# An encoder trunk: Strassen's seven products for most of the down projection, with the weight sums made in memory

## The chip, the cores and the metric

The kernel runs on one core of one Trainium2 chip. The metric is the device time of one execution in microseconds. One execution was profiled; the profile's times are counted from the start of its span.

## What is computed

Two layers of an encoder over 512 tokens of width 1024, in float32. Each layer is an attention and convolution half, an output projection, and a feed-forward half. The change is in the last line of the layer: the product of the gated activations (512 x 2816) with `w_down` (2816 x 1024).

```python
for l in range(DEPTH):                                  # DEPTH = 2
    h = rms_norm(x, pre_mix_norm[l])
    proj = jnp.einsum('bsd,de->bse', h, w_in[l])         # 1024 -> 3072: q, k, v, conv_u, gate_b, gate_c
    ...
    mix = jnp.einsum('bse,ed->bsd', merged, w_out[l])    # 1024 -> 1024
    x = x + rms_norm(mix, post_mix_norm[l])
    h = rms_norm(x, pre_ffn_norm[l])
    g, u = jnp.split(jnp.einsum('bsd,df->bsf', h, w_gate_up[l]), 2, axis=-1)   # 1024 -> 2 x 2816
    f = jnp.einsum('bsf,fd->bsd', jax.nn.silu(g) * u, w_down[l])               # 2816 -> 1024
    x = x + rms_norm(f, post_ffn_norm[l])
```

## The kernel before, in words

**Arithmetic.** Every float32 operand of a large product is split into a high part, rounded to the format that TensorE takes, and a low part, the rest. ScalarE (ACT) makes the high part with a copy and VectorE (DVE) the low part with a subtraction. A product is then three matmuls: high by high, high by low, low by high (`mm3`, L204 to L206).

**Weights.** They come from memory in an order fixed on the host, in chunks of 128 x 2048; half a chunk (128 x 1024, 512 KB) is the unit. `load_raw` (L117) loads a half into one of three "raw" buffers by SyncE's (SP's) queue. `split_half` splits it (ACT L177, DVE L178) into one of four pairs of buffers "wh" and "wl", after asking for the next two raw halves. `take` returns a half for use and splits up to two further ones.

**Order.** The program is traced under a planner. `tc.manual_schedule` holds only TensorE (PE) and SP to the order of the program. For ACT, DVE and GpSimd (POOL) the planner takes, at each moment of its own simulation, the instruction that stands first in the program among those whose inputs and buffers it believes to be ready; what comes out is a fixed list for each engine, which the chip runs in order, each instruction waiting for the semaphores that it needs. A few instructions are pinned with `keep_in_program_order` (the loading of ACT's tables, L119 and L235), and in the first stage ACT and DVE are held too.

**Stages of a layer.** (1) In-projection, with attention and convolution interleaved. Before it, in layer 0, `first_values` works with the first weights as they come: the loads stand in `LOADS`, positions, transposed x, weights, then x itself, whose squares (L543) give the norm (L222 and on); meanwhile POOL makes the angles of the rotary embedding from the positions (`rotary_values`, L285 to L315). In the attention and convolution steps, the square of each finished tile of 128 features is added to a running sum by POOL (L396), from a "tmp" tile, of which there are four; a convolution (`conv_tile`) holds two of them at once. (2) Out-projection: evacuations L674 to L678, norm, gain (L248), transposes into the next operand (L255 to L262). Here the first weights of the next stage are split by two DMAs of POOL's queue, a plain one (L189) and one that adds to what lies in the tile (L191). (3) Gate and up projections: 22 tiles of 128 hidden features; the first four by ordinary products, the other 18 by Strassen's seven products (`seven`, L815 to L855, its matmuls at L827 with 256 columns), whose weight sums DVE makes in SBUF (`prepare`). (4) Down projection: feature half f = 0, then 1; the contraction runs over 22 tiles m, for four token tiles t at once, with one bank of PSUM each; the last 4 (f = 0) or 8 (f = 1) tiles m run token tile by token tile, so that the evacuation of one (`evac`, ACT L918, DVE L920) lies under the matmuls of the next. Activations are split here (`split`, ACT L709, DVE L710), up to four tiles m ahead. With f = 1 the rest of the layer follows for each token tile: norm, residual (L643), the next layer's norm and gain, and the transposes of the first two token tiles (L255), placed three tiles m into the products of token tile t + 2.

**Buffers that matter here.** Eleven "big" tiles of 8 KB a partition, four "tmp", three "mid", two "gain", two "kl", and in PSUM four banks "acc", three "att", one "pv".

Of the kernel before, what the change touches and what calls it, by code (L numbers as in the profile page):

```python
# [16 lines left out]
F32 = mybir.dt.float32  # L17
# [13 lines left out]
MT = FFN // P  # L31
NCHUNK = 49
EPS = 1e-6
# [5 lines left out]
RAW_AHEAD, LOOK, WBUFS = 2, 2, 4  # L39

NDIRECT = 2

# [34 lines left out]
@with_exitstack  # L77
def encoder(ctx: ExitStack, tc: tile.TileContext, x, xT, pos, mask, cols, rows, w, out):
    nc = tc.nc
# [31 lines left out]
    def load_raw(i, c=0, d=1024):  # L111

        if i >= 2 * DEPTH * NCHUNK:
            return
        if i not in raws:
            raws[i] = sb.tile([P, 1024], F32, tag="raw", bufs=RAW_AHEAD + 1, name=nm("raw"))
        nc.sync.dma_start(raws[i][:, c:d], w[i // 2][:, (i % 2) * 1024 + c:(i % 2) * 1024 + d])  # L117

# [18 lines left out]

    def load_row(l, i):
        g = sb.tile([P, D], F32, tag="gain", bufs=2, name=nm("gain"))
        nc.sync.dma_start(g, rows[l, i].partition_broadcast(P))  # L140
        return g
# [38 lines left out]
    def split_by_dma(l, h):  # L180


        src = w[l * NCHUNK + 16][:, h * 1024:h * 1024 + 1024]
# [5 lines left out]
        nc.gpsimd.dma_start(hi, src)  # L189
        nc.scalar.activation(lo, hi.bitcast(F32), AF.Copy, scale=-1.0)  # L190
        nc.gpsimd.dma_start(lo, src, accum_op=ALU.add)  # L191
        halves[2 * (l * NCHUNK + 16) + h] = (hi, lo)

    def take(n, h, keep=None):


        i = 2 * n + h
# [355 lines left out]

    def in_proj_attention(l, hT, h, tables):

# [140 lines left out]

    def feed_forward(l, hT, hs, raw):
        base = l * NCHUNK + 16
# [7 lines left out]

        def split(m, src):
            hi, lo = act_dst(m)
            nc.scalar.copy(hi, src)  # L709
            nc.vector.tensor_sub(lo, src, hi.bitcast(F32))  # L710

        def unsplit(m):

            i = m - NDIRECT
            if i < 8:
                key, make, k = i // 4, lambda: big([P, 4, S]), i % 4
            elif i < 12:
                key, make, k = i // 2, lambda: sb.tile([P, 2, S], F32, tag="gain", bufs=2, name=nm("gain")), i % 2
            elif i < 18:
                key, make, k = i // 2, lambda: mid([P, 2, S]), i % 2  # L720
            else:
                key, k = i, 0
                make = lambda: sb.tile([P, 1, S], F32, tag="u" if i == 18 else "sqa", bufs=1, name=nm("u"))
            if key not in stage:
                stage[key] = make()
            return stage[key][:, k, :]

        def gated(m, gate, up):

            if m < NDIRECT:  # L730
                nc.vector.tensor_mul(gate, up, gate)
                split(m, gate)
            else:
                nc.vector.tensor_mul(unsplit(m), up, gate)

# [47 lines left out]
        def prepare(m):  # L783
# [23 lines left out]
            yield  # L807

        def down_splits():
            for k in (0, None, 1, None, 2, None):  # L810
                if k is not None:
                    split_half(2 * (l * NCHUNK + 38) + k)
                yield
# [83 lines left out]
        dbase = l * NCHUNK + 38  # L897
        fx = [[None] * NT for _ in range(2)]
# [3 lines left out]
        hs = [None] * NT  # L902
        done = set()

        def down(f, m, t, acc, keep=None):
            if m >= NDIRECT and m not in done:
                split(m, unsplit(m))
            done.add(m)
            u = f * MT + m
            wh, wl = take(dbase + u // 4, (u % 4) // 2, keep)  # L910
            c = (u % 2) * 512
            hi, lo = act_dst(m)
            mm3(acc, hi[:, t * P:(t + 1) * P], lo[:, t * P:(t + 1) * P], wh[:, c:c + 512], wl[:, c:c + 512],
                m == 0, m == MT - 1)

# [7 lines left out]
        for f in range(2):  # L923
            accs = [bank("acc") for _ in range(NT)] if f == 0 else [bank(g) for g in ("att", "att", "att", "pv")]
            tail = 4 if f == 0 else 8
            for m in range(MT - tail):
                if f == 0:
                    for k in range(m, min(m + 4, MT)):
                        if k >= NDIRECT and k not in done:
                            split(k, unsplit(k))  # L930
                            done.add(k)
                    if m == 14 - 3:
                        gpost = load_row(l, 3)
                        gnext = load_row(l + 1, 0) if l + 1 < DEPTH else None
                for t in range(NT):
                    down(f, m, t, accs[t])
            if f == 1 and gnext is not None:
                hT = new_hT()
            for t in range(NT):
                for m in range(MT - tail, MT):  # L940
                    if m == MT - tail + TURN_D and f == 1 and gnext is not None and t >= 2:
                        transposed(t - 2, hs[t - 2], hT, "acc")
                        hs[t - 2] = None
                    down(f, m, t, accs[t], 2 * dbase + (f * MT + MT - tail) // 2 if t < NT - 1 else None)
                evac(f, t, accs[t])
                if f == 0:
# [11 lines left out]
    with tc.manual_schedule(engines={mybir.EngineType.PE, mybir.EngineType.SP}):  # L958
# [4 lines left out]
        for l in range(DEPTH):  # L963
            merged, sq_a, sq_c, tables, inv = in_proj_attention(l, hT, hs, tables)
            hT, hs, raw = out_proj(l, merged, sq_a, sq_c, inv)
            hT, hs = feed_forward(l, hT, hs, raw)


def _weight_chunks(w_in, w_out, w_gate_up, w_down):

    out = np.empty((DEPTH * NCHUNK, P, 2048), np.float32)
    n = 0
    for l in range(DEPTH):
# [24 lines left out]
        wd = w_down[l].reshape(MT, P, 2, 512).transpose(2, 0, 1, 3).reshape(2 * MT, P, 512)  # L998
        for c in range(11):
            chunks.append(wd[4 * c:4 * c + 4].transpose(1, 0, 2).reshape(P, 2048))  # L1000
        for c in chunks:
            out[n] = c
            n += 1
    return out

# [44 lines left out]
```

## Time and profile before

| | us |
|---|---|
| median of 3 runs (1176.79 to 1177.01) | 1176.98 |
| the profiled execution, its own time | 1176.98 |
| its span | 1175.2 |
| TensorE (PE) busy | 1162.7 |
| weight loads (PEld) busy | 1025.1 |
| DVE busy | 784.0 |
| ACT busy | 630.0 |
| POOL busy | 41.6 |

A row of the page's groups, or of the same view for a stretch, reads: source line, engine, operation, output<-input by the program's names, shapes, count | busy time in us, mean ns of one | idle time of the engine ahead of them, and what ended most of it. The view of stretches gives, for each stretch, the busy time and number of instructions of PE, PEld, DVE, ACT and POOL, the granted TensorE clock, the mean busy share of the 16 DMA engines, and GB/s. A row of the timeline has the start, the duration, engine, line, and in brackets the idle time before it and what ended it. A row of DMA issues ends in the median time from issue to landing; a row of DMA queues has packets, MB, and the time that the packets took as a share of 16 engines. Matmuls overlap, so the mean of one (about 390 ns at 512 columns) is longer than the step from one to the next.

### The profile page before, as it was taken

The page shows a single profiled execution, that of the slowest core. Times are in us where ns is not written, and L with a number is a line of the kernel's source. Part 1 is how long each engine was busy: PE and PEld are TensorE (multiplying, and loading weights), DVE is VectorE, ACT ScalarE, POOL GpSimd, SP SyncE. Part 2 cuts the span into 40 slices and gives each one's busy share as a digit, 9 for nine tenths or more (in the row PEclk, how much of TensorE's full clock was granted, in tenths as well). Part 3 has the DMA queues.
Part 4 walks back from the last instruction along what each step waited for, and adds up shares of the span by engine and source line. Part 5 has one row for each costly group of instructions (what it writes and reads, how often), then busy time and mean ns, then how long its engine had stood idle before and what let it go on. Part 6 is the DMA issues. An engine that isn't in the chain of part 4 may idle for free.

```text
span 1175.2 us, 18024 instructions
## 1 busy us (share of the span) xinstructions
PE 1162.7 (99%) x7096; PEld 1025.1 (87%) x7096; DVE 784.0 (67%) x1326; ACT 630.0 (54%) x1217; POOL 41.6 (4%) x63
## 2 busy tenths in 40 slices
PE   9999999999999999999999999999999999999997
PEld 8777778899999999888877777788999999998886
DVE  5798655777888887432557986448778888883323
ACT  6677544654656557331445775437546555582211
POOL 6000011000000000000000000100000000000000
PEclk9999999999999999999999999999999999999999
DMA  8221234122333333423132212442133233334221
GB/s 321 90 72 54 73 94 135 60 73 90 108 108 102 99 107 116 154 74 118 42 106 92 72 55 73 128 123 71 38 108 106 95 106 108 108 126 125 90 72 72
DMA packets 33781, 116.48 MB, mean 99 GB/s; under 512 B 4000, under 2 KB 4000, under 8 KB 33696
## 3 DMA queue, kind: packets, MB, share of 16 engines
q1 hardware_dynamic: 31824, 110.05, 29.0%
q0 software_dynamic: 1152, 4.19, 1.6%
q8 instruction: 55, 0.90, 0.3%
q10 hardware_dynamic: 720, 1.09, 0.3%
q14 instruction: 30, 0.25, 0.1%
HBM read 113.22 MB, written 2.10 MB: 98 GB/s over the span
## 4 chain that ended last, share of the span: by engine, by line
PE 90%; DVE 4%; ACT 2%; POOL 2%; issue 2%; DVEq 0%; POOLq 0%
PE acc L827 18%; PE att L827 13%; PE acc L204 12%; PE acc L205 12%; PE acc L206 12%; PE att L204 4%; PE att L206 4%; PE att L205 4%; PE pv L441 3%; PE att L434 2%; PE att L417 1%; PE att L418 1%; PE pv L206 1%; PE pv L205 1%; PE pv L204 1%
## 5 line engine op out<-in xcount | busy, mean ns | idle before, releaser
L178 DVE TENSOR_TENSOR wl<-raw,wh 128x1024 fp32r<-128x1024 f32 x116 | 141.6, 1221 | 165.3 <-ACT wh L177 164.7
L177 ACT CAST wh<-raw 128x1024 fp32r<-128x1024 f32 x116 | 121.7, 1051 | 176.7 <-PE acc L206 67.4
L827 PE MATMUL acc<-big,wh 128*128 128x256 f32 x1152 | 212.0, 283 | 0.0
L827 PEld LDWEIGHTS acc<-big,wh 128*128 128x128 f32 x1152 | 179.8, 192 | 0.2
L827 PE MATMUL acc<-big,wl 128*128 128x256 f32 x576 | 163.0, 283 | 0.0
L827 PE MATMUL att<-big,wh 128*128 128x256 f32 x864 | 160.3, 283 | 0.0
L204 PE MATMUL acc<-big,wh 128*128 128x512 f32 (+1 forms) x400 | 154.1, 385 | 0.0
L206 PE MATMUL acc<-big,wl 128*128 128x512 f32 (+1 forms) x400 | 149.6, 374 | 0.0
L205 PE MATMUL acc<-big,wh 128*128 128x512 f32 (+1 forms) x400 | 149.3, 373 | 0.0
L827 PEld LDWEIGHTS att<-big,wh 128*128 128x128 f32 x864 | 134.7, 192 | 0.2
L827 PE MATMUL att<-big,wl 128*128 128x256 f32 x432 | 122.2, 283 | 0.0
L778 DVE TENSOR_TENSOR wl<-t,wh 128x1024 fp32r<-128x1024 f32 x72 | 88.0, 1222 | 42.7 <-ACT wh L777 42.7
L777 ACT CAST wh<-t 128x512 fp32r<-128x512 f32 x144 | 89.0, 619 | 47.6 <-PE att L827 31.7
L827 PEld LDWEIGHTS acc<-big,wl 128*128 128x128 f32 x576 | 110.6, 192 | 0.0
L204 PE MATMUL acc<-wh,big 128*128 128x512 f32 x272 | 106.6, 392 | 0.0
L205 PE MATMUL acc<-wl,big 128*128 128x512 f32 x272 | 106.0, 390 | 0.0
L206 PE MATMUL acc<-wh,big 128*128 128x512 f32 x272 | 105.9, 389 | 0.0
L204 PE MATMUL att<-wh,big 128*128 128x512 f32 x228 | 89.4, 392 | 0.0
L206 PE MATMUL att<-wh,big 128*128 128x512 f32 x228 | 88.8, 390 | 0.0
L205 PE MATMUL att<-wl,big 128*128 128x512 f32 x228 | 88.8, 389 | 0.0
L206 PEld LDWEIGHTS acc<-big,wl 128*128 128x128 f32 x400 | 75.3, 188 | 14.0
L204 PEld LDWEIGHTS acc<-big,wh 128*128 128x128 f32 x400 | 75.4, 189 | 12.3 <-issue 0.8
(238 smaller groups left out, 2100.8 us busy)
## 6 DMA issues: line engine op xcount, KB each, us to landing
raw<-in_w SPq DMA_DIRECT2D x188, 512.0 KB, 3.7
gain<-in_rows SPq DMA_DIRECT2D x7, 512.0 KB, 5.9
big<-in_xT SPq DMA_DIRECT2D x8, 256.0 KB, 5.3
raw<-in_w SPq DMA_DIRECT2D x8, 256.0 KB, 5.3
x<-in_x SPq DMA_DIRECT2D x4, 512.0 KB, 6.9
wk<-in_w POOLq DMA_DIRECT2D x4, 512.0 KB, 6.0
big<-in_w POOLq DMA_DIRECT2D x4, 512.0 KB, 4.9
out_dram<-x SPq DMA_DIRECT2D x4, 256.0 KB, 2.1
```

Source lines behind the costliest of these rows:

```text
L177: nc.scalar.copy(hi, raws[i])
L178: nc.vector.tensor_sub(lo, raws[i], hi.bitcast(F32))
L204: nc.tensor.matmul(o, sh, mh, start=start, stop=False)
L205: nc.tensor.matmul(o, sh, ml, start=False, stop=False)
L206: nc.tensor.matmul(o, sl, mh, start=False, stop=stop)
L417: nc.tensor.matmul(sc, qk[:, hd, q0:q0 + P], qk[:, 2 + hd, :], start=True, stop=False)
L418: nc.tensor.matmul(sc, qk[:, hd, q0:q0 + P], kl[:, hd, :], start=False, stop=True)
L434: nc.tensor.transpose(tp[:, k * P:(k + 1) * P], sm[:, k * P:(k + 1) * P], ident)
L441: nc.tensor.matmul(o[hd * 64:hd * 64 + 64, half * 256:half * 256 + 256], V[:, k, hc:hc + 64], PT[hd][:, k, :], start=k == 0, stop=k == NT - 1)
L777: nc.scalar.copy(hi[:, c:c + 512], src[:, c:c + 512])
L778: nc.vector.tensor_sub(lo[:, :n], src[:, :n], hi[:, :n].bitcast(F32))
L827: nc.tensor.matmul(o[:, :HS], sh[:, c], mh[:, k, :], start=start and k == 0 and n == 0, stop=k == 3 and n == 2, skip_group_check=True)
```

## The change

The 22 contraction tiles of the down projection are divided: tiles 0 to 15 go by Strassen's scheme in Winograd's form, tiles 16 to 21 (`REST` = 6) as before. The 16 tiles make a product of a 2 x 2 block of activations (token half by contraction half) with a 2 x 2 block of weights b11, b12, b21, b22 (contraction half by feature half). Seven products of 8 tiles, for 2 token tiles each, replace eight; each is `partial`, 8 x 2 x 3 matmuls of 512 columns. The ones after the first add to banks into which ACT or DVE has copied an earlier result; `written` runs a matmul on a bank ahead of such a copy.

- **Weights.** `w_down` gets an array of its own, `wd`, laid out by quarters. A layer has 34 halves for the down projection instead of 22: 28 for the products (`SB`), six for the rest. Four of the seven products take sums of weight quarters, t1 = b11 + b12, t3 = b12 + b22, t2 = t1 + b22, t4 = t2 + b21, which are read from a tensor in memory, `tsum`.
- **Sums.** `weight_sums` makes them by 16 DMAs a layer from memory to memory, of 1 MB each, issued by POOL: eight copies and eight with `accum_op=add`. It is a generator: the program takes one step of it in every eighth `advance` of the attention stage, one after each of the 18 gate/up tiles, and what is left after the last.
- **Activations.** `gated` no longer splits tiles 0 and 1 at once; all tiles are kept unsplit (`place`). For each product `operands` makes the sum of activation quarters where one is needed (four of seven, DVE), the high part (ACT) and the low part (DVE), in three pieces, under the product before; the first set under the last gate/up tile, with the first weight splits. Tiles 16 to 21 are split under the seventh product.
- **The end.** After the seven products the eight banks hold both feature halves; the six remaining tiles are added token tile by token tile, 18 matmuls each, with the evacuation, norm and transposes as before.
- **Gains.** `gpost` and `gnext` are loaded at the head of the stage, into the "kl" tiles, not at its eleventh tile.

```diff
+    tsum = [dpool.tile([P, 4, KS * 512], F32, tag=f"tsum{l}", name=f"tsum{l}") for l in range(DEPTH)]
...
+    def weight_sums(l):
+        b11, b12, b21, b22 = (down_quarter(l, g, f) for g in range(2) for f in range(2))
+        t1, t2, t3, t4 = (tsum[l][:, k, :] for k in range(4))
+        for pairs in (((t1, b11), (t3, b12)), ((t1, b12), (t3, b22)), ((t2, t1),), ((t2, b22),), ((t4, t2),), ((t4, b21),)):
+            for n, (o, src) in enumerate(pairs):
+                for c in range(0, KS * 512, 2048):
+                    add = {"accum_op": ALU.add} if src is b22 or src is b21 or (src is b12 and o is t1) else {}
+                    nc.gpsimd.dma_start(o[:, c:c + 2048], src[:, c:c + 2048], **add)
+                    yield
...
         def advance():
+            if count[0] % 8 == 7:
+                next(adding, None)
...
         for m in range(SEVEN, MT):
             ahead = prepare(m + 1) if m + 1 < MT else down_splits()
             seven(m, ys[m % 2], ahead)
+            next(adding, None)
+        for _ in adding:
+            pass
...
+        def operands(p):
+            hi_t, lo_t = seconds[p] = [big([P, KS, HS], F32R) for _ in range(2)]
+            if p == 1:
+                s1.append(big([P, KS, HS]))
+            for k, n in ((0, 4), (4, 2), (6, 2)):
...
+                if p in (1, 2, 4, 5):
...
+                    nc.vector.tensor_tensor(o, x, y, op)
+                    yield
+                hi = hi_t[:, k:k + n, :]
+                nc.scalar.copy(hi, o)
+                nc.vector.tensor_sub(lo_t[:, k:k + n, :], o, hi.bitcast(F32))
+                yield
...
+        def partial(p, outs, start, ahead):
+            hi_t, lo_t = seconds.pop(p)
+            for k in range(KS):
+                wh, wl = take_half(d0 + p * (KS // 2) + k // 2)
+                c = (k % 2) * 512
+                for i in range(2):
+                    st = slice(i * P, i * P + P)
+                    for n, (sh, mh) in enumerate(((hi_t, wh), (hi_t, wl), (lo_t, wh))):
+                        nc.tensor.matmul(outs[i], sh[:, k, st], mh[:, c:c + 512], start=start and k == 0 and n == 0,
+                                         stop=False, skip_group_check=True)
+                next(ahead, None)
...
+        partial(0, c11, True, operands(1))
+        c21.extend(written("acc", 1) for _ in range(2))
+        for i in range(2):
+            nc.scalar.copy(c21[i], c11[i])
+        partial(1, c12, True, operands(2))
...
+        for i in range(2):
+            nc.scalar.copy(p5[i], c12[i])
+        partial(2, c21, False, operands(3))
+        for i in range(2):
+            nc.scalar.copy(u2[i], c21[i])
+        partial(3, c11, False, operands(4))
+        partial(4, c21, False, operands(5))
+        c22.extend((written("att", 5), written("pv", 5)))
+        for i in range(2):
+            nc.vector.tensor_sub(c22[i], p5[i], c21[i])
+        partial(5, c12, False, operands(6))
+        for i in range(2):
+            nc.vector.tensor_sub(c12[i], c12[i], u2[i])
+        partial(6, c21, False, rest_splits())
+        accs = [c11 + c21, c12 + c22]
...
             for t in range(NT):
-                for m in range(MT - tail, MT):
-                    if m == MT - tail + TURN_D and f == 1 and gnext is not None and t >= 2:
+                for m in range(2 * KS, MT):
+                    j = f * REST + m - 2 * KS
+                    if m == 2 * KS + TURN_D and f == 1 and gnext is not None and t >= 2:
                         transposed(t - 2, hs[t - 2], hT, "acc")
```

More of the change, by code (lines that the diff above doesn't have):

```diff
@@ L39 @@
 RAW_AHEAD, LOOK, WBUFS = 2, 2, 4
-NDIRECT = 2
 SEVEN = 4
@@ L77, in encoder @@
 @with_exitstack
-def encoder(ctx: ExitStack, tc: tile.TileContext, x, xT, pos, mask, cols, rows, w, out):
+def encoder(ctx: ExitStack, tc: tile.TileContext, x, xT, pos, mask, cols, rows, w, wd, out):
     nc = tc.nc
@@ L705, in act_dst, with split, place @@
             return acth[m // 2][:, m % 2, 0, :], acth[m // 2][:, m % 2, 1, :]
-        def split(m, src):
+        def split(m):
             hi, lo = act_dst(m)
+            src = unsplit(m)
             nc.scalar.copy(hi, src)
             nc.vector.tensor_sub(lo, src, hi.bitcast(F32))
-        def unsplit(m):
[L714 to L726, printed above, removed]
-        def gated(m, gate, up):
[L730 to L734, printed above, removed]
+        def place(m):
+            if m < 12:
+                key, make, k = m // 4, lambda: big([P, 4, S]), m % 4
+            elif m < 16:
+                key, make, k = m // 2, lambda: sb.tile([P, 2, S], F32, tag="gain", bufs=2, name=nm("gain")), m % 2
+            else:
+                key, make, k = m // 2, lambda: mid([P, 2, S]), m % 2
+            if (m < 12, key) not in stage:
+                stage[m < 12, key] = make()
+            return stage[m < 12, key], k
+        def unsplit(m):
+            tile_, k = place(m)
+            return tile_[:, k, :]
+        def gated(m, gate, up):
+            nc.vector.tensor_mul(unsplit(m), up, gate)
         def gated_full(m, accs):
@@ L807, in prepare, with half_of @@
             yield
+        seconds = {}
+        s1 = []
+        def half_of(m, n, f):
+            tile_, k = place(m)
+            return tile_[:, k:k + n, f * HS:f * HS + HS]
+        def operands(p):
[3 more added lines that the diff above has]
+            for k, n in ((0, 4), (4, 2), (6, 2)):
+                a11, a21, a12, a22 = (half_of(g * KS + k, n, f) for g in range(2) for f in range(2))
+                o = (a11, s1 and s1[0][:, k:k + n, :], s1 and s1[0][:, k:k + n, :], a12, a21,
+                     s1 and s1[0][:, k:k + n, :], a22)[p]
+                if p in (1, 2, 4, 5):
+                    x, y, op = {1: (a21, a22, ALU.subtract), 2: (o, a11, ALU.subtract),
+                                4: (a11, a21, ALU.subtract), 5: (a12, o, ALU.add)}[p]
+                    nc.vector.tensor_tensor(o, x, y, op)
[4 more added lines that the diff above has]
+                yield
         def down_splits():
-            for k in (0, None, 1, None, 2, None):
+            first = operands(0)
+            for k in (None, 0, None, 1, None, 2):
+                next(first, None)
                 if k is not None:
-                    split_half(2 * (l * NCHUNK + 38) + k)
+                    split_half(2 * (l * NCHUNK + NW) + k)
                 yield
@@ L902, in feed_forward @@
         hs = [None] * NT
[L903 to L914, printed above, removed]
+        gpost = load_row(l, 3, "kl")
@@ new lines, in feed_forward @@
+        gnext = load_row(l + 1, 0, "kl") if l + 1 < DEPTH else None
+        accs = [[bank("acc"), bank("acc")], []]
+        (c11, c12), c21, c22 = (accs[0], [bank("att"), bank("att")]), [], []
+        def partial(p, outs, start, ahead):
[9 more added lines that the diff above has]
+                next(ahead, None)
+            for _ in ahead:
+                pass
@@ new lines, in rest_splits, with written @@
+        def rest_splits():
+            for m in range(2 * KS, MT):
+                split(m)
+                yield
+        def written(tag, p):
+            b = bank(tag)
+            hi, lo = take_half(d0 + p * (KS // 2))
+            nc.tensor.matmul(b, seconds[p][0][:, 0, :P], hi[:, :512], start=True, stop=True)
+            return b
+        partial(0, c11, True, operands(1))
+        c21.extend(written("acc", 1) for _ in range(2))
+        for i in range(2):
+            nc.scalar.copy(c21[i], c11[i])
@@ new lines, in feed_forward @@
+        partial(1, c12, True, operands(2))
+        p5 = [tmp([P, S]) for _ in range(2)]
+        u2 = [tmp([P, S]) for _ in range(2)]
+        for i in range(2):
[8 more added lines that the diff above has]
+            nc.vector.tensor_sub(c22[i], p5[i], c21[i])
@@ L923, in feed_forward @@
         for f in range(2):
[L924 to L936, printed above, removed]
             if f == 1 and gnext is not None:
@@ L1003, in _weight_chunks @@
             n += 1
-    return out
+    return out, down
 def _columns(attn_out_norm, conv_out_norm, conv_w, pre_mix_norm):
@@ L1040 @@
         "in_rows": np.stack([a["pre_mix_norm"], a["post_mix_norm"], a["pre_ffn_norm"], a["post_ffn_norm"]], axis=1),
-        "in_w": _weight_chunks(a["w_in"], a["w_out"], a["w_gate_up"], a["w_down"]),
+        "in_w": weights,
+        "in_wd": down,
     }
```

65 lines of the change are left out of this document (48 added, 17 removed).

## The prediction

> **What bounds the kernel now.** I read the page's first two parts, then the stages as stretches of time, then single stages.
>
> ```profile
> PE 1162.7 (99%) x7096; PEld 1025.1 (87%) x7096; DVE 784.0 (67%) x1326; ACT 630.0 (54%) x1217; POOL 41.6 (4%) x63
> ...
> PEclk9999999999999999999999999999999999999999
> ...
> 285.00:466.60 181.60, 181.60 (x1514) 181.49 (x1513) 146.23 (x198) 110.69 (x239) 0.00 (x0) 1.00 0.33 105
> 466.60:590.00 123.40, 123.40 (x554) 102.33 (x553) 53.89 (x88) 45.73 (x82) 0.00 (x0) 1.00 0.30 98
> ...
> 1048.60:1175.20 126.60, 119.74 (x529) 98.79 (x527) 46.80 (x71) 35.60 (x58) 0.00 (x0) 0.98 0.29 92
> ...
> 470.00:560.00 90.00, 90.00 (x399) 74.53 (x398) 31.09 (x41) 26.21 (x37) 0.00 (x0) 1.00 0.35 115
> ```
>
> TensorE is never without work at full clock. The first three rows of stretches are layer 0's gate/up products and the two down projections (columns: stretch, its length, busy time and count of PE, PEld, DVE, ACT, POOL, clock, DMA share, GB/s). In the down stage DVE is busy 54 of 123 us. Inside it, 399 matmuls in 90.00 us give **0.2256 us each**. So time goes only if matmuls go or TensorE waits.
>
> **What is removed.** Before, a layer's down projection is 22 tiles x 4 token tiles x 2 feature halves x 3 = 528 matmuls. After, seven products of 8 tiles x 2 banks x 3 = 336, four matmuls that first write a bank, and 6 x 8 x 3 = 144 for the other tiles: 484. Less: 44 x 0.2256 = 9.93 us a layer, **-19.9 us** in all. That is the largest gain the change can give, unless some present stall goes; the stage shows none (123.40 of 123.40).
>
> **Feeding the seven products.** Weights must be split 28 times (each product its own 4 halves) where the 16 tiles took 16.
>
> ```profile
> L178 DVE TENSOR_TENSOR wl<-raw,wh 128x1024 fp32r<-128x1024 f32 x23 | 28.1, 1223 | 59.1 <-ACT wh L177 59.0
> ...
> L710 DVE TENSOR_TENSOR big<-mid,big 128x512 fp32r<-128x512 f32 x6 | 3.8, 684 | 0.0
> ...
> L177 ACT CAST wh<-raw 128x1024 fp32r<-128x1024 f32 x22 | 23.2, 1053 | 62.2 <-PE acc L206 32.0 <-PE pv L206 30.1
> ...
> L709 ACT CAST big<-mid 128x512 fp32r<-128x512 f32 x6 | 3.3, 616 | 0.0
> ...
> L918 ACT ACTIVATE row<-acc 128x512 f32<-128x512 f32 x4 | 2.4, 598 | 6.1 <-PE acc L206 6.1
> ...
> raw<-in_w SPq DMA_DIRECT2D x17, 512.0 KB, 3.6
> gain<-in_rows SPq DMA_DIRECT2D x2, 512.0 KB, 6.4
> ```
>
> An operand set is three pieces (1024, 512, 512 columns): on DVE 1.223 + 2 x 0.684 = 2.59 us for its low part and as much again for its sum, which four of seven need; on ACT 1.053 + 2 x 0.616 = 2.29. DVE over the products: 28 x 1.223 = 34.2, low parts 7 x 2.59 = 18.1, sums 4 x 2.59 = 10.4, four combinations of banks x 0.69 = 2.7, six late splits 4.1; less the first set, made in the last gate/up step: **67 us**. ACT: 29.5 + 16.0 + six bank copies 3.6 + 3.7 = 53. TensorE needs 340 x 0.2256 = 76.7. So it stays the bound on average, but in a product whose successor needs a sum DVE has 4.9 + 5.2 = 10.1 of 10.8 us, and it also waits for ACT (59 us of idle in the first row came from there).
>
> The loads: a half now feeds 12 matmuls, 2.71 us, where it fed 24. Three raw buffers turn over in at least 3.6 (load) + 1.05 + 1.22 and some 0.3 of signals = 6.2 us, against 3 x 2.71 = 8.1; a busy DVE may add one op of 1.2 and ACT another 1.05, and nothing is left. The two gain rows (6.4 us to land) now load at the head of the stage, between the first halves. Lower bound of all this: 0. Upper bound: each of four tight products late by 10.1 + one op of 1.2 + the raw turn's remainder, some 1.5 us, and 2 us for the gain rows: 8 us a layer. I take 2.5 a layer, nearer to 0, as DVE can work ahead (four weight buffers; free big tiles for a second operand set): **+5 us**.
>
> **The turn into layer 1.** Gains and transposes follow a finished token tile.
>
> ```profile
> 570.56 0.19 ACT L918 ACTIVATION_READ_ACCUMULATOR row<-att 128x1 f32 x1
> ...
> 575.37 1.29 DVE L248 SCALAR_TENSOR_TENSOR mid<-x,small,gain 128x1024 f32<-128x1024 f32 x1
> ...
> 577.36 1.03 PE L255 MATMUL acc<-ident,mid 128*128 128x128 f32 x8
> ```
>
> From the square's start, 0.6 before the first row, the chain takes to 576.66, 6.7 us. TensorE had 24 + 9 matmuls, 7.4 us, to get there; now 18 + 9, 6.1 us. It waits 0.6, and the next tiles, 4.1 us apart with some 4.5 us of DVE work each, about as much again: **+1.5** (0 to 4), in layer 0 alone.
>
> **The sums in memory.** A layer has 16 DMAs of 1 MB on POOL's queue, 8 copies and 8 adds. Their price, and where POOL issues them:
>
> ```profile
> 129.97:136.00 6.03, 6.03 (x32) 5.01 (x32) 4.68 (x12) 4.52 (x11) 0.78 (x1) 1.00 0.57 175
> ...
> q0 software_dynamic: 144, 0.52, 30.1%
> q1 hardware_dynamic: 144, 0.52, 25.7%
> ...
> q0 software_dynamic: 144, 0.52, 37.8%
> ```
>
> The first q0 row is the copy of 512 KB issued at 129.97 (share of 16 engines in 129.9:136): 0.301 x 6.1 = 1.84 us of all engines, 1.9 over the two. The second is an add of 512 KB (182:190): 0.378 x 8 = 3.02, the other window gave less, so about 2.85. For 1 MB: 3.8 and 5.7. These went between memory and SBUF; memory to memory may be a half dearer (an add reads twice there and writes) or no dearer. A layer's sums: 8 x 3.8 + 8 x 5.7 = **76 us of all DMA engines**, 152 for both. In most places that is spare: the share is about 0.3.
>
> Now the order on POOL.
>
> ```profile
> 1.06 0.28 POOL masks.py:199 TENSOR_SCALAR_AFFINE_SELECT ident<-ident 128x128 f32<-128x128 f32 x1
> 7.72 0.63 POOL L285 CAST small<-pos_sb 128x4 f32<-128x4 int32 x1 [6.38 <-DMA pos_sb<-in_pos]
> ...
> 114.14 1.52 POOL L396 TENSOR_TENSOR sqa<-sqa,tmp 128x512 f32<-128x512 f32 x1 [86.03 <-ACT tmp L395]
> 129.97 0.78 POOL L189 DMA_DIRECT2D wk<-in_w  x1 [14.31 <-PE att L418]
> 142.16 1.28 POOL L396 TENSOR_TENSOR sqa<-sqa,tmp 128x512 f32<-128x512 f32 x1 [11.41 <-ACT tmp L395]
> 153.49 1.34 POOL L396 TENSOR_TENSOR sqc<-sqc,tmp 128x512 f32<-128x512 f32 x1 [10.04 <-ACT tmp L395]
> ...
> L674 ACT ACTIVATE tmp<-acc,small x8: 681/686/690, 196.7 to 783.8; 128x512 f32<-128x512 f32 x8
> ```
>
> L189 stands in the program behind the first L674 (196.7) and behind all of L396's adds of that layer. POOL issued it at 129.97, ahead of five of them, the moment its tile came free. Only PE and SP are held to program order. The sums write memory of their own and wait for no tile; so the places that the change gives them should not hold, and POOL should issue them at the first idle time, from 1.34 us, while it waits 6.38 us for the positions: at 0.6 us of POOL a plain DMA there is room for several. What they meet there:
>
> ```profile
> 6.00:9.00 3.00, 3.00 (x14) 2.57 (x14) 1.71 (x3) 2.07 (x4) 1.17 (x2) 1.00 1.00 355
> ...
> 24.00:27.00 3.00, 3.00 (x15) 2.49 (x14) 0.40 (x2) 1.46 (x4) 2.49 (x9) 1.00 0.99 388
> ...
> 30.00:33.00 3.00, 3.00 (x15) 2.49 (x14) 1.89 (x7) 1.08 (x3) 0.00 (x0) 1.00 0.00 0
> ...
> 60.00:233.00 173.00, 172.90 (x881) 137.69 (x880) 121.36 (x264) 101.03 (x195) 11.90 (x10) 1.00 0.28 83
> ...
> L543 ACT ACTIVATE mid<-x x4: 1060/1062/1063, 18.3 to 24.1; 128x1024 f32<-128x1024 f32 x4
> ...
> 28.40 1.28 ACT L235 ACT_TABLE_LOAD   x1
> 29.70 0.30 ACT L222 ACTIVATE small<-small,eps_sb 128x4 f32<-128x4 f32 x1
> ```
>
> From 6 to 27 us the DMA engines are full (1.00, 0.99). The last tile of x lands at 24.0 and its square ends at 25.2; the norm waits until 29.7 for POOL's rotary chain and a table load, so x has 4.5 us to spare. Each copy of 1 MB in front delays x by 3.8: two cost 3, three 7, four 11; eight at an even share of the engines with the loads would bring x at about 45 us, a cost of 16. None in front costs nothing. I take three, since a planner that believes the positions land earlier than at 7.7 fills the gap with that many: **+7 us** (0 to 16). The other queue rows say that the two queues share one set of engines: 30.1% + 25.7% makes the 0.57 of the stretch. The Trainium skill, "DMA: Bandwidth & Descriptors", section "Issuing engines are not separate DMA queues", says the same: DMAs of all issuing engines interleave on the same 16. By that rule the start pays; were POOL's DMAs on engines of their own, the sum below would be 7 us lower.
>
> From 27 us to the down stage the sums run beside loads at a share of 0.28. A half there serves some 5.4 us of TensorE, so a landing of 6 or 7 us instead of 3.6 still fits three buffers; POOL's own adds come a little late. **+1** (0 to 30; the upper end is the second rival).
>
> **Sum.** -19.9 + 5 + 1.5 + 7 + 1 = -5.4. The profiled execution took 1176.98 us (span 1175.2 and 1.8 around it), which is also the median of the three runs: 1171.6, so **1172 us**. This case's own range is 1164 to 1180.
>
> **Rivals.** (1) *The sums run where the program has them*, one in eight steps of the attention and one a gate/up tile. Then the start keeps its time: -19.9 + 5 + 1.5 + 1 = -12.4, **1164 us** (1157 to 1169). For it: the code spaces them. Against it: L189 above. Chance 0.22.
>
> (2) *POOL's queue jams, and the kernel is slower.* An add waits for the landing of the copy that it adds to, and POOL takes its queue in order, so L396's adds stand behind every sum that was put ahead of them. With both layers' sums in front, 152 us of engines less some 15 by 27 us, at 1 - 0.28 of the engines, end near 27 + 137 / 0.72 = 217 us, while L396 is due at 114, 142 and 153. Each late one keeps one of four tmp tiles; with three kept, the next convolution, which needs two at once, stops DVE's queue at about 165, and with it the softmax and the weight splits. If POOL comes free at 190 the stop is 25 us, and the sum is -5.4 + 25: **1196 us** (1182 to 1205). It decides from the point where POOL's queue clears later than about 165; a planner that prices the DMAs as the chip does would interleave the adds and escape. Chance 0.23. The Trainium skill, same page, section "Two DMAs through the same engine are not ordered", asks for just such a wait on the issuing engine; the wait of POOL itself shows in the last column of its rows, and no run here shows one for an earlier sum.
>
> (3) *The products are fed too slowly*, DVE or the raw buffers being the bound in most of the seven: 8 us a layer instead of 2.5: -5.4 + 11 = **1183**, or 1176 with nothing in front; about **1178 us**. For it: 10.1 of 10.8. Against it: in the gate/up products DVE had 146 of 181.6 us without delaying TensorE. Chance 0.10.
>
> **Numbers.** The forecast has 0.45. A measurement tells 0.2%, 2.4 us, from no change: 1174.6 to 1179.3 is the same. The forecast's own range falls 0.27 faster, 0.11 same, 0.07 slower; rival 1 all faster; rival 2 all slower; rival 3 0.02, 0.05, 0.03. Faster 0.51, same 0.16, slower 0.33. The range of all: from 1159, which leaves out the best of rival 1, to 1194, half of rival 2.
>
> **What would show it.** The profile after should have 88 matmuls fewer. Right: POOL rows of the sums before 7 us, a later L543 and L222 by some 7 us, and gaps of PE of a few us in each down stage, released by DVE. Rival 1: the sums' rows spread up to some 400 us and the start unchanged. Rival 2: L396 late by tens of us and DVE waiting for POOL. Wrong altogether: a down stage that is not about 10 us shorter while the start is unchanged, or sums that land after layer 0's down projection has begun.

## The result, and the profile after

The changed kernel takes 1243.72 us (median of four runs, 1242.51 to 1245.10), against 1176.97 before: a ratio of 1.0568, with a 95% interval of 1.055 to 1.0586. The forecast was 1172 and its range ended at 1194. The profiled execution after took 1242.51 us, with a span of 1240.7.

The stretches show where the time is. First the start, then layer 0's seven products and its other tiles with the turn, then layer 1's seven products (columns as in the rows of before):

```profile
0.00:27.00 27.00, 23.42 (x93) 19.29 (x94) 11.06 (x17) 11.59 (x17) 12.18 (x26) 0.94 0.89 335
27.00:60.00 33.00, 17.23 (x64) 12.92 (x63) 2.48 (x3) 7.64 (x11) 5.10 (x12) 0.81 1.02 291
60.00:112.00 52.00, 0.00 (x0) 0.00 (x0) 4.19 (x8) 2.33 (x3) 14.20 (x29) 0.50 1.01 279
...
548.00:624.00 76.00, 76.00 (x338) 62.92 (x337) 61.33 (x68) 47.88 (x60) 0.00 (x0) 1.00 0.67 207
624.00:660.00 36.00, 33.46 (x154) 27.34 (x153) 20.91 (x46) 15.53 (x39) 0.00 (x0) 1.00 0.27 85
1128.00:1204.00 76.00, 76.00 (x337) 62.92 (x337) 59.38 (x65) 45.87 (x56) 0.00 (x0) 1.00 0.67 199
```

TensorE does nothing at all from 60 to 112 us, while the DMA engines are full. In the seven products it is never without work; the 2.5 us that are missing from 624 to 660 are the turn into layer 1.

POOL's first square add of each layer marks the stages. The last row is layer 1's before the change; layer 0's stood at 114.14.

```profile
195.72 1.51 POOL L437 TENSOR_TENSOR sqa<-sqa,tmp 128x512 f32<-128x512 f32 x1 [37.98 <-ACT tmp L436]
...
771.66 1.52 POOL L437 TENSOR_TENSOR sqa<-sqa,tmp 128x512 f32<-128x512 f32 x1 [494.47 <-ACT tmp L436]
```

```profile
696.15 1.52 POOL L396 TENSOR_TENSOR sqa<-sqa,tmp 128x512 f32<-128x512 f32 x1 [500.50 <-ACT tmp L395]
```

Up to layer 0's first square add the kernel has lost 81.6 us; at layer 1's the loss is 75.5, so layer 0 has given back 6.1; at the end it is 65.5, so layer 1 has given back 10.0. Nearly the whole loss is in the first 115 us, and the gain that was reckoned is there behind it.

What happens at the start stands in POOL's list (the sums are L155, the rotary chain L326 to L356; the bracket is the idle time before the row and what ended it):

```profile
1.32 0.72 POOL L155 DMA_DIRECT2D tsum<-in_wd  x1 [0.32 <-issue]
...
25.01 0.82 POOL L155 DMA_DIRECT2D tsum<-in_wd  x1 [3.70 <-DMA tsum<-in_wd]
...
29.86 0.89 POOL L155 DMA_DIRECT2D tsum<-in_wd  x1 [3.36 <-DMA tsum<-in_wd]
30.49 0.55 POOL L343 TENSOR_TENSOR ang<-ang,small 128x32 f32<-128x32 f32 x1
...
99.37 0.92 POOL L155 DMA_DIRECT2D tsum<-in_wd  x1 [9.19 <-DMA tsum<-in_wd]
...
114.17 0.22 POOL L356 TENSOR_SCALAR ang<-ang 128x32 f32<-128x32 f32 x1
```

The planner put a sum into nearly every gap between two instructions of the rotary chain. From L334 on each row of the chain takes 0.2 to 0.7 us, but an add that stands ahead of it waits until the copy it adds to has landed, and POOL works its list in order. The chain's last row, at 27.90 before, comes at 114.17. POOL's waits up to 115 us, summed (us in total, times, longest):

```profile
POOL tsum L155 <- DMA tsum<-in_wd: 41.7, 11, 9.2
POOL mid L367 <- ACT mid L584: 19.9, 3, 11.2
POOL tsum L155 <- DMA tsum<-tsum: 9.4, 3, 4.3
```

So 51.1 us of the chain's 86 are waits for earlier sums. Another 19.9 are three memsets that stand in the same list and wait for a tile that the squares of x free, and x is late: its last square starts at 57.3 (24.1 before).

```profile
L584 ACT ACTIVATE mid<-x x4: 1057/1059/1063, 34.5 to 57.3; 128x1024 f32<-128x1024 f32 x4
```

```profile
q0 software_dynamic: 1296, 9.44, 56.2%
q1 hardware_dynamic: 3820, 9.15, 41.6%
...
x<-in_x SPq DMA_DIRECT2D x4, 512.0 KB, 30.9
```

These three rows are the DMA view of 1 to 60 us: the sums (q0) hold 56% of all engines and the loads (q1) the other 42%.

From here two ways lead to TensorE, both over ACT's list. First ACT's rows, then two of TensorE's waits:

```profile
46.97 1.06 ACT L584 ACTIVATE mid<-x 128x1024 f32<-128x1024 f32 x1 [11.30 <-DMA x<-in_x]
...
48.02 1.03 ACT L216 CAST wh<-raw 128x1024 fp32r<-128x1024 f32 x1
...
108.90 0.23 ACT L354 ACTIVATE sn<-ang 128x32 f32<-128x32 f32 x1 [45.35 <-POOL ang L351]
114.42 0.23 ACT L357 ACTIVATE cs<-ang 128x32 f32<-128x32 f32 x1 [5.29 <-POOL ang L356]
...
115.97 0.30 ACT L263 ACTIVATE small<-small,eps_sb 128x4 f32<-128x4 f32 x1
```

```profile
PE att L382 <- DVE small L264: 60.7, 1, 60.7
PE att L245 <- ACT wh L216: 10.3, 1, 10.3
```

The shorter wait is x's lateness: the cast of a weight half (L216) stands behind a square that waits for x, and TensorE waits for it until 49.10. The longer one is the chain's. ACT's sine and cosine wait for POOL, DVE copies them into the rotary tables (114.69 to 115.13), and TensorE's next matmuls in its order are the transposes of these tables (L382), which start at 115.27. (The profile puts the wait of the matmuls down to L264, DVE's row right behind the copies, and the wait of the same transposes' weight loads, 61.1 us, to L356, the chain's last row.) The norm of x (L263) needs nothing of the chain, but stands behind the cosine on ACT and comes at 115.97 instead of 29.70. TensorE waits only 0.6 us more for what follows from it. The first of these transposes ran at 36.5 before, so it is 78.8 us late: 60.7 of them are the stop, and 18.1 had been lost ahead of it.

### The profile page after: what moved, and what is told of

Read it like the earlier page. It is cut to its first block, busy times and chain, and to the rows that moved or that the text cites. A ratio compares the mean times of both kernels' runs of the same rounds, so it can differ in the third digit from the quotient of the medians.

```text
span 1240.7 us, 18112 instructions
## 1 busy us (share of the span) xinstructions
PE 1149.5 (93%) x7008; PEld 1011.3 (82%) x7008; DVE 848.3 (68%) x1392; ACT 671.6 (54%) x1263; POOL 59.5 (5%) x95
## 3 DMA queue, kind: packets, MB, share of 16 engines
q0 software_dynamic: 5760, 37.75, 11.8%
## 4 chain that ended last, share of the span: by engine, by line
PE 84%; DMA 8%; DVE 3%; ACT 2%; issue 1%; POOL 0%; SPq 0%; DVEq 0%; ACTq 0%
PE acc L897 17%; PE att L897 13%; PE acc L991 9%; PE acc L245 8%; PE acc L246 8%; PE acc L247 8%; PE att L991 4%; DMA tsum<-in_wd 3%; DMA x<-in_x 3%; PE acc L1053 3%; PE pv L482 3%; PE att L475 2%; PE att L245 2%; PE att L247 2%; PE att L246 2%; PE att L458 1%
## 5 line engine op out<-in xcount | busy, mean ns | idle before, releaser
L217 DVE TENSOR_TENSOR wl<-raw,wh 128x1024 fp32r<-128x1024 f32 x140 | 171.3, 1223 | 102.5 <-ACT wh L216 101.5
L216 ACT CAST wh<-raw 128x1024 fp32r<-128x1024 f32 x140 | 147.3, 1053 | 112.4 <-PE acc L246 36.2
L897 PEld LDWEIGHTS acc<-big,wh 128*128 128x128 f32 x1152 | 179.8, 192 | 0.2
L991 PE MATMUL acc<-wh,big 128*128 128x512 f32 x320 | 99.5, 389 | 0.0
L817 ACT CAST wh<-raw 128x512 fp32r<-128x512 f32 x108 | 63.6, 621 | 46.1 <-PE acc L897 31.2
L245 PEld LDWEIGHTS acc<-big,wh 128*128 128x128 f32 x400 | 75.4, 189 | 12.4 <-issue 0.8
L246 PEld LDWEIGHTS acc<-big,wh 128*128 128x128 f32 x400 | 75.6, 189 | 11.6
L818 DVE TENSOR_TENSOR wl<-raw,wh 128x512 fp32r<-128x512 f32 x72 | 68.8, 956 | 21.5 <-ACT wh L817 21.4
L897 PEld LDWEIGHTS att<-big,wl 128*128 128x128 f32 x432 | 82.9, 192 | 0.0
L991 PEld LDWEIGHTS acc<-wh,big 128*128 128x128 f32 x320 | 60.1, 188 | 12.4
## 6 DMA issues: line engine op xcount, KB each, us to landing
tsum<-in_wd POOLq DMA_DIRECT2D x24, 1024.0 KB, 12.4
```

The costliest lines, as they stand in the source:

```text
L216: nc.scalar.copy(hi, raws[i])
L217: nc.vector.tensor_sub(lo, raws[i], hi.bitcast(F32))
L245: nc.tensor.matmul(o, sh, mh, start=start, stop=False)
L246: nc.tensor.matmul(o, sh, ml, start=False, stop=False)
L817: nc.scalar.copy(hi[:, c:c + 512], src[:, c:c + 512])
L818: nc.vector.tensor_sub(lo[:, :n], src[:, :n], hi[:, :n].bitcast(F32))
```

## The experiments

Nine kernels were run. The lines are those of the changed kernel unless said. A run with one time only has no interval.

### Placing the sums: e1, e3, e4

e1 holds every sum to its place in the program.

```diff
-                    nc.gpsimd.dma_start(o[:, c:c + 2048], src[:, c:c + 2048], **add)
+                    tc.keep_in_program_order(nc.gpsimd.dma_start(o[:, c:c + 2048], src[:, c:c + 2048], **add))
```

> Each sum is pinned behind what the program has issued on POOL before it, so none runs ahead of the rotary chain. Theory (the sums, floated to the front of POOL's queue, hold up the rotary chain and nothing else costs much): the start keeps its time, 1243.7 - 82 = about 1161 us, faster than before by 1.3%. Rival (the products are fed too slowly, or sums beside the loads cost time wherever they run): 1170 us or more.

1171.79 us, ratio to before 0.9952 (0.9934 to 0.997). The 72 us that came back show that the place of the sums is the cause; the last ten that were expected did not come. The stretch 200 to 260 us and two of TensorE's waits:

```profile
200.00:260.00 60.00, 53.52 (x286) 46.09 (x285) 42.83 (x90) 31.03 (x74) 7.25 (x10) 0.94 0.83 239
```

```profile
PE acc L245 <- ACT big L303: 4.2, 1, 4.2
...
PE att L539 <- POOL sqc L437: 3.0, 2, 1.6
```

The program has the sums spread over the attention, but an add must wait for its copy, and so nine of layer 0's, and three of layer 1's behind them, bunch between 181 and 230 us, beside the output projection and its weight loads. There DMA is 0.83 busy, where it was 0.25 before, TensorE has 53.5 us of work instead of 59.3, and its clock is 0.94. The wait of 4.2 lies behind a raw half of the first gate/up weights, for which ACT waits 6.9 us until 248.73, after layer 1's three. By the first square adds (layer 1's at 699.14, in e2 below at 689.56) layer 0 has lost 9.4 against e2; layer 1's nine sums bunch in the same way, with none behind them, and cost 1.8.

e3 holds only the adds, on the theory that only they make POOL wait.

```diff
+                    ins = nc.gpsimd.dma_start(o[:, c:c + 2048], src[:, c:c + 2048], **add)
+                    if add:
+                        tc.keep_in_program_order(ins)
```

> Only the adds are pinned; the eight copies from w_down (8 MB, which wait for nothing) still run at the front, one between two rotary instructions. Theory that the loss is POOL waiting for landed copies and sums: no wait is left at the front, the start loses only some 5 us of POOL's issue time, about 1166 us. Rival that the loss is the DMA engines shared with the first loads: x lands some 28 us late as it did in the changed kernel (57 us for 24), about 1189 us.

1213.19 us: neither. The copies from the weights still fill the DMA engines at the start (the first square add comes at 138.26), and the pinned adds now stand ahead of POOL's own loads of the first gate/up weights (L228), in both layers. The first row is TensorE's wait for it; the others, from the chain of waits, how it came about in layer 0 (lines behind L155 are two higher in this kernel):

```profile
PE acc L247 <- DVE tmp L533: 23.0, 2, 11.9
```

```profile
195.84 17.69 DMA tsum<-in_wd
213.53 0.29 issue
213.82 0.53 POOL tsum L155
...
216.23 12.38 DMA big<-in_w
228.67 0.92 issue
229.59 1.04 ACT wh L218
```

POOL waits for a sum, so its load of a weight half starts late and lands late beside the sums; ACT stands in its list at that half's negation, and the splits and the convolution on DVE come behind.

e4 leaves the sums free, but behind the last instruction of the rotary chain.

```diff
+                    ins = nc.gpsimd.dma_start(o[:, c:c + 2048], src[:, c:c + 2048], **add)
+                    tc.add_manual_dep(ins.ins, last[0].ins.name, ..., reason="after rotary")
...
-        nc.gpsimd.tensor_scalar(a, a, -1.0, float(np.pi / 2), op0=ALU.mult, op1=ALU.add)
+        last.append(nc.gpsimd.tensor_scalar(a, a, -1.0, float(np.pi / 2), op0=ALU.mult, op1=ALU.add))
```

> All sums are held behind the last rotary instruction, and are free after it; POOL's list then has 28 of 32 sums ahead of the first square add. The start keeps its time by both theories. If the second rival of the prediction has the place right (square adds late, tmp tiles kept, DVE stopped from about 165 us until POOL is free near 190 to 200), 1161 + 25 = about 1186 us. If the square adds have slack enough, about 1161 to 1165 us.

1189.14 us. The start is whole, and the sums of both layers run from 27 to 172 us. The first square add, due at 114, comes at 153.95, and TensorE waits in the attention. Stretches 60:112 and 112:200, and then waits of PE, DVE and ACT (lines three higher here):

```profile
60.00:112.00 52.00, 52.00 (x281) 40.57 (x280) 46.43 (x105) 40.00 (x76) 6.49 (x11) 1.00 0.99 279
112.00:200.00 88.00, 64.18 (x321) 48.57 (x320) 38.13 (x83) 32.17 (x61) 15.94 (x19) 0.86 0.89 236
```

```profile
PE att L478 <- DVE row L472: 16.1, 1, 16.1
PE pv L485 <- ACT mid L479: 7.7, 1, 7.7
```

```profile
DVE tmp L525 <- POOL sqa L440: 8.5, 1, 8.5
```

```profile
ACT wk L231 <- DMA wk<-in_w: 16.8, 1, 16.8
```

The stop of DVE for a square add, by which the second rival worked, is there, with 8.5 us. The larger one is the mechanism of e3: POOL's load of gate/up weights is issued at 172.47, behind the last sum (130 before), and lands at 185.4, with ACT's list standing at it for 16.8 us. By place and size the two are TensorE's 7.7 and 16.1. And the first row holds a thing that was not expected: DMA engines 0.99 busy for 52 us, and TensorE without a gap.

### The engines or the queue: e5

e5 moves the rotary chain from POOL to DVE, its first part three pieces of weights later. Of the start's two causes only the sharing of the DMA engines is left.

```diff
-FIRST = ["f0 w0 f1 w1 r", "f2 w2", "f3 w3", "f4 w4", ...]
+FIRST = ["f0 w0 f1 w1", "f2 w2", "f3 w3", "f4 w4 r", ...]
...
-        nc.gpsimd.tensor_scalar(k, a, float(1.0 / (2 * np.pi)), MAGIC, op0=ALU.mult, op1=ALU.add)
+        nc.vector.tensor_scalar(k, a, float(1.0 / (2 * np.pi)), MAGIC, op0=ALU.mult, op1=ALU.add)
```

> The rotary chain runs on DVE, whose order is fixed there, instead of on POOL; the sums float to the front as in the changed kernel. Theory that the loss is the rotary chain behind waiting sums in POOL's queue alone: about 1165 us. Rival that the shared DMA engines cost the start as well: x lands 28 to 33 us late and the norm waits for it, about 1189 to 1194 us.

1190.67 us, the rival's number, but only half by the rival's path, so that the match is in part luck. The last square of x still starts at 55.2, and the norm comes at 58.81:

```profile
L584 ACT ACTIVATE mid<-x x4: 1044/1056/1059, 46.4 to 55.2; 128x1024 f32<-128x1024 f32 x4
```

```profile
PE acc L245 <- ACT wh L579: 17.9, 4, 8.4
```

TensorE does not wait for that norm. It waits 17.9 us for the splits of the first weights, which land late too, and a little for their low parts; the last of these waits ends at 48.34, and its clock is 0.79 up to 27 us and 0.81 from there to 60. The transposes of the rotary tables then come at 64.61 without a wait, 28 later than before.

Late loads alone therefore cost 29 us against the version without that cost (1161.41, e9 below), and 53 more in the changed kernel (1243.72 - 1190.67) go with POOL's list. The changed kernel's own trace divides the loss a little differently, into 18 ahead of TensorE's stop and 61 in it. The split is not clean, as POOL, freed of the chain, issued four copies by 4 us where it had issued one, and DVE has the chain's work on top of its own.

The run also bounds how late a square add may come. The first stands at 172.38, some 30 us later than its stage, itself 28 late, has it due, and from 112 to 200 us TensorE works 87.90 of 88 us. In e4 it was 40 late, and TensorE waited.

### What the products are worth without the sums: e2

```diff
-            adding = weight_sums(l)
+            adding = iter(())
```

The products of t1 to t4 load plain quarters instead, so their values differ and their work does not.

> The sums' DMAs are left out; the weights of the products t1 to t4 are loaded from plain quarters instead, so the values are not the reference's, while every load and matmul stays. Theory (the seven products themselves gain the 19.9 us of their matmuls, feeding them costs nothing, and the turn into layer 1 costs the 4.2 us by which the transposes L296 waited longer in e1_pinned): 1176.8 - 19.9 + 4.2 = 1161 us. Rival (the ten us that were missing in e1_pinned are lost in the products' stage, not by the sums): 1170 us or more.

1160.63 us, ratio 0.9866 (0.9851 to 0.9881). That is the change without any price of the sums, and e1's missing ten were theirs.

### Looking for a place: e6, e7, e8, e9

e6 puts a layer's 16 sums into the first 16 of the 18 late gate/up steps; a one-column copy on POOL of that step's fifth product makes POOL really wait for the step.

```diff
-            if count[0] % 8 == 7:
-                next(adding, None)
...
             nc.scalar.copy(p5, q[:, :HS])
+            tc.keep_in_program_order(nc.gpsimd.tensor_copy(small(1), p5[:, :1]))
+            next(adding, None)
```

> No sum is issued in the attention any more; each of a layer's 16 sums is pinned in the gate/up stage behind a one-column copy on POOL of that step's fifth product, so POOL really waits for the step. Theory (the sums cost only where POOL has other work or the loads have no slack): 1161 to 1163 us, no wait of TensorE between 180 and 235 us, clock 1.00 there, and the first square add at 113.9. Rival (37 MB of extra traffic costs wherever it runs): 1168 to 1172 us, the ten us of e1_pinned again, as waits for weight splits inside the gate/up products.

1194.2 us (1188.06 to 1202.07), ratio 1.0148 (1.0094 to 1.0202): worse than the rival expected, by the rival's mechanism. (The sums are 33.6 MB; the expectation's 37 is all that POOL's queue moves.) First a group of the gate/up matmuls in e6, then the same without sums (e2); last, DVE's wait for raw weights in 288:480 of e6, which was 0.5 in the same place before:

```profile
L895 PE MATMUL acc<-big,wl 128*128 128x256 f32 x576 | 166.3, 289 | 18.2 <-DVE wl L816 18.2
```

```profile
L897 PE MATMUL acc<-big,wl 128*128 128x256 f32 x576 | 163.0, 283 | 0.0
```

```profile
L833 DVE TENSOR_TENSOR t<-raw,t 128x512 f32<-128x512 f32 x16 | 11.1, 692 | 34.5 <-DMA raw<-in_w 34.4
```

A sum every ten us, DMA only 0.64 busy in this stretch, and it still hurts: these steps consume a raw half as soon as it lands. Beside the 18 us of waits TensorE is also busy 14.1 us longer with the same matmuls (1156.5 against 1142.4 us).

e7 is e6 with the transposes of the turn two tiles later (TURN_D 5 instead of 3).

> As e6_gate_up, and the transposes of a finished token tile are put two tiles (1.35 us each) later in the shorter loop of the rest (TURN_D 5 instead of 3). Theory (the turn's 5 us of waits L296 are the chain of the norm against a loop that became shorter): 2 to 4 us less than e6_gate_up, 1158 to 1160 us, and the waits of L296 on DVE under 1.5 us in all. Rival (the wait only moves on to the first products of layer 1, which need the transposed tiles): the same time as e6_gate_up within 0.5 us.

1197.45 us (1192.66 to 1203.72), ratio 1.0178 (1.0138 to 1.0217), its median inside e6's spread, and the waits of L296 add up to 4.3 instead of 5.0 us. Of layer 0's three at the turn (1.39, 1.21, 2.11) one is gone, one is 1.05, and the last, ahead of layer 1's first products, has grown to 2.95: most of the wait moved on, as the rival said. On the time this run is inconclusive.

e8 takes up e4's unexpected row: all 16 sums of a layer in one pinned burst at the head of its attention, ahead of the first square add, which is not due for 80 us.

```diff
-            if count[0] % 8 == 7:
-                next(adding, None)
...
+        tc.keep_in_program_order(nc.gpsimd.tensor_copy(small(1), V[:, 0, :1]))
+        for _ in adding:
+            pass
         qks = [None] * 4
```

> All 16 sums of a layer are pinned in one burst at the head of that layer's attention, behind a one-column copy on POOL of the first tile of V, so behind the rotary chain and ahead of the first square add. Theory (the sums are free where nothing of POOL's falls due for 85 us and the weight loads of the stage have slack even at full DMA engines, as in the stretch from 28 to 114 us of e4_after_rotary, where TensorE did not wait): 1161 to 1163 us, the same as e2_no_sums within 2 us; the first square adds no later than some 5 us and no wait of TensorE for them. Rival (full DMA engines cost TensorE some us wherever they last for 85 us, as in e6_gate_up): 1166 us or more, with waits for weight splits in the attention, or clock under 1.00 there.

1172.2 us, ratio 0.9963 (0.9949 to 0.9977). Half right. Layer 0's burst (first row) cost nothing: without the sums, e2 has 28.56 us of work in that stretch, and its first square add, at 113.74, is 0.5 ahead of e8's. Layer 1's (second row) cost some eleven (its first square add comes at 701.27, in e2 at 689.56), mostly as one wait of the first scores for a q/k tile; in e2 the stretch has 59.35 us of work:

```profile
30.00:60.00 30.00, 28.45 (x134) 22.97 (x133) 24.08 (x50) 18.46 (x31) 6.22 (x10) 1.00 0.91 283
...
600.00:660.00 60.00, 50.39 (x230) 40.05 (x230) 34.92 (x68) 28.04 (x46) 7.22 (x10) 0.91 1.01 282
```

```profile
PE att L458 <- ACT big L420: 9.0, 2, 8.5
```

Layer 0 has loaded six halves of weights before its burst starts; layer 1 has only its three raw buffers, and a half took 12.2 us to land there. e9 only moves layer 1's burst behind the first q/k tile:

```diff
         def advance():
+            if l == 1 and count[0] == 0:
+                burst(qks[0][0][:, 0, :1].bitcast(F32))
```

> Layer 0 as e8_head_burst; layer 1's burst is pinned behind the first q/k tile instead of the first tile of V, so some 35 us later, when the first scores already have what they need. Theory (the 9 us of waits and the lower clock of e8_head_burst came from the head of layer 1 alone, where the weights of the V and first q/k products have no loads in hand; layer 0's burst cost nothing): 1161 to 1163 us, the wait of TensorE for the q/k tile L420 back at 0.4 us, the first square add of layer 1 up to 5 us late without a wait of TensorE. Rival (a burst in layer 1 costs its ten us wherever it starts): 1168 to 1172 us.

**1161.41 us** (1160.99 to 1163.54), ratio to before 0.9873 (0.9855 to 0.9891): faster than both kernels, and 0.8 us from the version without sums. The two bursts, and the weight loads beside the first (30 to 114 us):

```profile
28.00:114.00 86.00, 84.54 (x433) 66.81 (x432) 72.35 (x160) 61.64 (x113) 11.36 (x18) 1.00 0.95 267
625.00:712.00 87.00, 86.34 (x454) 67.68 (x453) 72.49 (x164) 63.16 (x121) 11.28 (x16) 1.00 0.94 261
```

```profile
raw<-in_w SPq DMA_DIRECT2D x12, 512.0 KB, 10.6
```

The wait for the q/k tile is back at 0.4 us. In the kernel before, the same two stretches have 84.51 and 86.36 us of TensorE's work at a DMA share of 0.23 and 0.19. The sums are free here, although a weight half takes 10.6 us to land instead of 3.7. Layer 1's burst only just fits: POOL issues its last sum at 693.10, and the first square add follows at 693.65, 4.1 later than in e2, without a wait of TensorE.

## Why the prediction was wrong, point by point

**What failed: "I take three".** The step "I take three, since a planner that believes the positions land earlier than at 7.7 fills the gap with that many: +7 us (0 to 16)" is the one. It had seen that the sums would float to the front of POOL's list. But it took the rotary chain as one block that the sums stand ahead of ("the norm waits until 29.7 for POOL's rotary chain"), and counted only what they do to x. The planner fills every gap it sees, so the sums went between the chain's instructions, and the chain waited for landings. This term was put at nothing; it cost about 53 us by e5 and 61 by TensorE's stop. The part that was priced came out too small as well, and by more than x: late loads cost 29 us in e5, there as waits for the first weights and not for the norm, and 18 ahead of the stop in the changed kernel, rather than 7. The upper bound of 16 let eight sums in front bring x at 45 us; nine sums, all issued by 36 us, with 56% of the engines up to 60, brought its last square at 57.

The Trainium skill, "DMA: Bandwidth & Descriptors", section "Issuing engines are not separate DMA queues", has the DMAs of all issuing engines interleave on the same 16; the trace agrees, as the two queues' 56.2% and 41.6% make up one full set of engines. The Trainium skill, same page, section "Two DMAs through the same engine are not ordered", has the issuing engine wait for the earlier DMA; the trace agrees, with POOL's 51.1 us above.

**The second rival had the mechanism but not the place.** It said that sums queued on POOL block what stands behind, and put the blocked work at L396, at 25 us. In e4 the sums stand there, and TensorE's two long waits are 24 us; but only the 7.7 go with the square adds (DVE's 8.5), the 16.1 with POOL's own weight load (L228, L189 before), which the rival did not name. The same load is what e3 waits for, in both layers. In the changed kernel the first thing behind the sums was the rotary chain, so the rival's 1205 was also too low. Between POOL's list and TensorE there were two more: ACT's sine and cosine, and DVE's copies into the rotary tables.

**The gain was right.** 88 matmuls fewer: layer 1, with nothing else in it, is 10.0 us shorter, and -9.93 a layer was predicted.

**Feeding the products: 0, not +5.** TensorE is busy 76.00 of 76.00 us in both layers' products. DVE had 61.3 us of work in layer 0's (67 reckoned, over 76.7), and no product had to wait for its 10.1 of 10.8. The third rival falls with it.

**The turn: about +4, not +1.5.** In e9 the transposes of the turn (571 to 600 us) wait 4.6 us in three waits, where the kernel before has 0.8. This is the upper end of the range given, 0 to 4. With it the sum becomes -19.9 + 0 + 3.8 = -16.1, so 1160.9; e2 measured 1160.63 and e9 1161.41.

**The price of a sum was close.** q0 has 11.8% of 1240.7 us, 146.4, and 18.8 of that are the DMAs that it had before (1.6% of 1175.2): 127.6 us for 32 sums, where 152 was estimated. 

```profile
q0 software_dynamic: 5760, 37.75, 11.8%
```

The amount of DMA work alone did not decide: e9 moves the same bytes.

**"Sums beside loads later": +1 held only by place.** The same traffic cost 0.8 us in the two stretches of e9, eleven in e1 and e8, and 34 in e6's gate/up stage (each against e2's 1160.63). The prediction read the spare capacity from the mean share of DMA; what decides, as far as the places of the waits show, is how many weights a stage has in hand when a load comes late. No run changed the number of buffers, so that stays argued.

**The first rival** (sums where the program has them, 1164) is e1: 1171.79, outside its 1157 to 1169, as the adds' waits bunch the sums beside the output projection and, in layer 0, up to the first gate/up weights.

## What to carry to other kernels

A DMA that waits for another DMA is, on its engine's list, an instruction of the length of that landing: whatever the planner puts behind it is late by so much, and so is what stands behind that on the next engine. When work is added to an engine that looks idle, list what is due on it and when, pin the new work, and tie it by a real dependency to a stretch that is long enough. Spare DMA share does not say that a stretch can take more traffic; look there for how late a load may land before an engine waits for it.

## What was not expected of the hardware

- From 28 to 114 us of e9 the DMA engines were 0.95 busy and the weight loads' landing (30 to 114) rose from 3.7 to 10.6 us without any loss of TensorE's time; in e6 a mean share of 0.64 with landings of 4.7 us in the median cost 18 us of waits.
- A lower clock followed stops of TensorE of only about 3 us. In e6 twelve waits make 18.2 us, and the granted clock of 288 to 480 us is 0.97. It is not low throughout, but right behind the two stops of 3.0 us, which end at 352.87 and 410.14; from 452 to 456 us, with waits of 1.6 and 0.9, it is 1.00. Layer 1 has the same behind stops of 3.5 and 2.9 us (0.79 in 956 to 964, 0.57 in 1004 to 1008). Together these stretches lack some 8.5 us of full clock, which is part of the 14.1 above; the rest stays open. In the long stop of the changed kernel (60 to 112 us) the clock was 0.50. The Trainium skill, "TensorE: Matmul & The Clock Gate", section "What's actually happening", has the half clock come after an idle window of about 3.4 us; the stops here, 2.9 to 3.5 us by the profile, lie close to that.

```profile
288.00:480.00 192.00, 181.90 (x1458) 179.49 (x1457) 136.31 (x188) 105.92 (x228) 19.09 (x34) 0.97 0.64 181
```

```profile
352.00:360.00 8.00, 7.13 (x37) 7.13 (x38) 6.34 (x9) 1.00 (x3) 0.00 (x0) 0.57 0.88 244
408.00:416.00 8.00, 5.86 (x36) 5.86 (x37) 7.39 (x11) 1.52 (x4) 0.00 (x0) 0.79 0.88 244
```

- A sum from memory to memory is no dearer than the transfers into SBUF were: 127.6 us over 32 sums is 4.0 us of all engines for 1 MB, where the transfers of 512 KB before were reckoned at 1.9 for a copy and 2.85 for an add. Its landing is longer than that: the 24 that read the weights took 12.4 us in the median in the changed kernel and 8.2 in e6, where a sum was issued about every ten us.
